# Feed-forward and output products turned around: operand stationary, weights moving in 512 columns

## The chip, the cores and the metric

The kernel runs on one core of a Trainium2 chip. The core has TensorE (PE in the profile, with its weight loads shown as PEld), VectorE (DVE), ScalarE (ACT), GpSimd (POOL) and SyncE (SP, which here only issues DMAs). Times are device microseconds. The kernel before took 1064.02 us, the median of 3 runs (1062.18 to 1064.86). "Faster" and "slower" below mean against that median.

## The reference

A two-layer decoder trunk over 256 tokens of width 1024, all in float32:

```
x = x + 0.5 * ffn(rmsnorm(x))          # f0
x = x + mamba2_mixer(rmsnorm(x))       # ssm: 32 heads, output product y @ w_out (2048 x 1024)
x = x + 0.5 * ffn(rmsnorm(x))          # f1
k, v = kv(rmsnorm(x))                  # shared keys and values
x = x + 0.5 * ffn(rmsnorm(x))          # f2
x = x + attention(rmsnorm(x), k, v)    # window 128, 16 heads; out @ w_o (1024 x 1024) + b_o
x = x + 0.5 * ffn(rmsnorm(x))          # f3
out = rmsnorm(x)
ffn(h) = (silu(h @ w_gate) * (h @ w_up)) @ w_down      # 1024 -> 2816 -> 1024
```

The weight of each norm is folded into the operand that the next product reads; the factor 1/sqrt(mean square + eps) of each token, called rs, is multiplied in after the product.

## The kernel before

Every weight matrix is cut into units of 512 KB, 128 rows by 1024 numbers, in one fixed order (`ORDER`). There are 341 of them: each of the four feed-forwards has 22 gate, 22 up and 22 down units, the mixer 41 input and 16 output units (`so`), the attention 8 query, 2 value and 8 output units (`ao`), and the keys take 2. `Weights` (lines 110 to 183) streams them: SP loads chunks of two units into four buffers, ACT rounds each unit to float32r (`hi`, line 144), and DVE takes the remainder (`lo`, line 155). Six buffers hold the parts, and `ahead` (line 168) keeps four units ready beyond the one in use. The activations are split in the same way, so each product is three: hi by hi, hi by lo, lo by hi.

Activations are kept transposed, with columns on partitions and the 256 tokens along the free dimension: the residual is eight tiles `X` of 128 by 256. In `unit` (line 334, the matmul at 344) and `rows` (line 353, matmuls at 361 to 363) a 128x128 block of the weights is the stationary operand and 256 tokens move, so that a unit is 24 matmuls of 256 columns. In `ffn` (line 456) a gate and an up unit share a PSUM bank; `evac` multiplies by rs (broadcast over partitions), applies SiLU, multiplies and splits into `hh`, `hl` (lines 470 to 479). A down unit follows four tiles later (`LAG`), accumulating into four banks.

`Slots` (line 185) holds the order of the side work by hand: after every unit `tick` runs what was put at that slot, then splits more weights. Each engine runs its instructions in the program's order. The last two units of a product go column tile by column tile in `tail` (line 506), and `next_stage` (line 367) follows each tile with the residual (line 381, or 379 with the attention's bias), the next operand's split (lines 383 and 373) and the squares (line 291, summed on POOL at 294). `stage_norm` (line 449) then sums the squares on TensorE (line 304), takes the root on POOL (lines 313 to 317) and spreads it over partitions with a diagonal (lines 324, 329, 331). `finish` (line 424) is the last norm. In the attention, `rope` (line 802) uses rs, DVE and two POOL operations (815 and 818), and `restack` moves the result by eight DMAs on SP's queue before the scores (line 885) can run; line 966 transposes the probabilities.

Of the kernel before, what the change touches and what calls it, by code (L numbers as in the profile page):

```python
# [9 lines left out]
F32 = mybir.dt.float32  # L10
# [6 lines left out]
P = 128  # L17
# [4 lines left out]
LAG = 4  # L22
SLACK = 2
# the mixer's plan, in slots: by group, by pair of head tiles
# [14 lines left out]
def ffn_order(l, i):  # L39
    o = []  # L40
    for f in range(NF):
        o += [("g", l, i, f), ("u", l, i, f)]
        if l == 1 and i == 0 and f == 5:
            o += [("kA",), ("kB",)]
        if f >= LAG:
            o.append(("d", l, i, f - LAG))
    return o + [("d", l, i, f) for f in range(NF - LAG, NF)]

# [31 lines left out]
# columns of the packed small parameters  # L80
SM = {}
_n = 0
for _name, _w in [
    ("convw", 96), ("convb", 24), ("snw", 16), ("sd", 16),
    ("dtb", 32), ("alog", 32), ("bk", 2), ("bq", 8), ("bo", 8), ("sink", 16), ("bv", 256),
]:
    SM[_name] = (_n, _n + _w)
    _n += _w
NSM = _n

# columns of the norms' weights
NO = {"norm": 0, "kvn": 48, "fin": 56}
NNO = 64

# columns of the constants
# [14 lines left out]
class Weights:  # L110
    """The stream of weight units: loaded in chunks, split into two parts that float32r holds exactly."""
# [56 lines left out]
    def ahead(self, n):  # L168
        """Both parts of the next n units, and the high part of one more."""
# [46 lines left out]
class Trunk:  # L216
    def __init__(self, ctx, tc, a):
# [12 lines left out]
        xp = [cp.tile([P, 2, T], F32, name=f"X{k}") for k in range(KT // 2)]  # L230
        self.X = [xp[k // 2][:, k % 2] for k in range(KT)]
        self.xh = [cp.tile([P, T], F32R, name=f"xh{k}") for k in range(KT)]
        self.xl = [cp.tile([P, T], F32R, name=f"xl{k}") for k in range(KT)]
# [9 lines left out]
        def first(t):  # L243
            q, h = nc.sync.dma_start, D // 2
            q(self.norms, a["norms"])
            q(xp[0], a["x"][:, 0:2, :])
            q(t[:, 0, :h], a["w"][0, :, 0, :h])
            q(xp[1], a["x"][:, 2:4, :])
            q(xp[2], a["x"][:, 4:6, :])
            q(t[:, 0, h:], a["w"][0, :, 0, h:])  # L250
            q(xp[3], a["x"][:, 6:8, :])
            for i in range(1, CH):
                q(t[:, i, :], a["w"][0, :, i, :])

        self.norms = cp.tile([P, NNO], F32, name="norms")
        self.W.load(first)
        self.W.load()
        nc.sync.dma_start(self.co, a["const"])
        self.W.load()
        nc.sync.dma_start(self.sm, a["small"])  # L260
        for _ in range(RAW - 3):
            self.W.load()
        self.ident = self.cc("ident")
        self.slots = Slots()

# [12 lines left out]
    def bank(self, name):  # L278
        return self.ps.tile([P, 512], F32, tag="pp", name=name)

    def accs(self, name):
        return [self.ps.tile([P, 512], F32, tag="acc", name=f"{name}{b}") for b in range(4)]
# [14 lines left out]
    def rs_stats(self, accs, n, key):  # L297
        """1/sqrt(mean + eps) of each token, tokens on partitions; then as diagonals for rs_spread."""
# [3 lines left out]
        for t in range(2):  # L302
            for i, acc in enumerate(accs):
# [3 lines left out]
                )  # L307
        v = wk.tile([P, 2], F32, tag="v", name=f"v_{key}")
        y = wk.tile([P, 2], F32, tag="y", name=f"y_{key}")
        q = wk.tile([P, 2], F32, tag="nt", name=f"nt_{key}")  # L310
        G = nc.gpsimd
        nc.vector.tensor_scalar(v, b[:, 256:258], 1.0 / n, EPS, ALU.mult, ALU.add)
# [5 lines left out]
        return b, y  # L318
# [15 lines left out]
    def unit(self, what, out, xh=None, xl=None, before=None):  # L334
        """A column tile of a product: out[128 columns, tokens] from all eight row tiles."""
        nc = self.nc
        xh = self.xh if xh is None else xh
        xl = self.xl if xl is None else xl
        hi, lo = self.W.next(what)
        passes = [(k, w, x) for k in range(KT) for w, x in ((hi, xh), (hi, xl), (lo, xh))]  # L340
        if self.W.pos == 1:
            passes = [(k, w, x) for w, x in ((hi, xh), (lo, xh), (hi, xl)) for k in range(KT)]
        for n, (k, w, x) in enumerate(passes):
            nc.tensor.matmul(out, w[:, k * P : (k + 1) * P], x[k], start=n == 0, stop=n == len(passes) - 1)  # L344
        if before:
            before()
        self.tick()

# [4 lines left out]
    def rows(self, units, accs, first, last, done=None):  # L353
        """Row tiles of a product, accumulated over all eight column tiles; units: (weights' parts, hh, hl)."""
        nc = self.nc
        for j in range(KT):
            out = accs[j % 4][:, (j // 4) * T : (j // 4) * T + T]
            s = slice(j * P, (j + 1) * P)
            for n, ((hi, lo), hh, hl) in enumerate(units):
                f, e = first and n == 0, last and n == len(units) - 1  # L360
                nc.tensor.matmul(out, hi[:, s], hh, start=f and j < 4, stop=False, skip_group_check=True)  # L361
                nc.tensor.matmul(out, lo[:, s], hh, start=False, stop=False, skip_group_check=True)  # L362
                nc.tensor.matmul(out, hi[:, s], hl, start=False, stop=e, skip_group_check=True)  # L363
            if done:
                done(j, out)

    def next_stage(self, key, scale, wcol, bias=None):
# [9 lines left out]
        def done(j, out):  # L377
# [7 lines left out]
            if j > 0:  # L385
                fin(j - 1)
# [814 lines left out]
```

## Time and profile before

| | |
|---|---|
| median of 3 runs | 1064.02 us |
| the profiled execution's span | 1060.6 us |
| what lies around the span, from the median | 3.4 us |
| TensorE busy, matmuls recorded | 1042.4 us (98%), 8690 |
| VectorE, ScalarE, GpSimd busy | 713.7, 563.9, 79.7 us |
| read from HBM | 187.27 MB, 178 GB/s over the span |
| TensorE's mean granted clock | 0.996 |

The profiled execution has no separate time of its own beside its span; the difference to the median is taken as constant. Busy time of TensorE is modelled, since matmuls are pipelined: a record lasts longer than the distance to the next one. What one matmul costs in a stream is therefore read from the distance between starts, not from its duration. A plain float32 matmul leaves two records, a float32r matmul and a transpose one.

### The profile page before, as it was taken

Reading aid. Unit: us, or ns where it says so; the run is one execution under the profiler, and the core shown is the slowest. Engines: PE = TensorE matmul, PEld = TensorE weight load, DVE = VectorE, ACT = ScalarE, POOL = GpSimd, SP = SyncE. Lnnn points to the kernel's source line nnn. Section 1 sums busy time; section 2 is a strip of 40 time slices with the busy share of each in tenths; the row PEclk is TensorE's granted clock in tenths of the full one; section 3 lists DMA queues with packets and bytes.
Section 4 is the critical chain, followed back from the end, with each engine's and each line's share of the span. In section 5 each row is a group of like instructions: output and inputs, shape, how many; then the busy total and the mean of one; then the engine's idle time right before and its main releaser. Section 6 shows DMA issues by size and latency. Waiting matters only on the chain.

```text
span 1060.6 us, 20911 instructions
## 1 busy us (share of the span) xinstructions
PE 1042.4 (98%) x8690; PEld 1027.5 (97%) x8690; DVE 713.7 (67%) x1245; ACT 563.9 (53%) x930; POOL 79.7 (8%) x122
## 2 busy tenths in 40 slices
PE   8999999999999999999999999999999999999996
PEld 8999999999999999999999999999998899999996
DVE  4755555789999967655556775555589776555554
ACT  6544444669796755444445654444465764444443
POOL 3000000210111111000000200000022020000000
PEclk9999999999999999999999999999999999999998
DMA  8545555457545455455545454555444244555521
GB/s 329 204 170 191 194 191 186 159 180 271 183 151 198 162 193 187 174 190 193 193 166 205 154 200 177 192 190 191 173 178 160 102 159 163 196 181 189 193 94 40
DMA packets 30142, 191.02 MB, mean 180 GB/s; under 512 B 3904, under 2 KB 5728, under 8 KB 8544
## 3 DMA queue, kind: packets, MB, share of 16 engines
q1 hardware_dynamic: 30048, 189.69, 49.0%
q8 instruction: 68, 1.11, 0.4%
q14 instruction: 26, 0.21, 0.1%
HBM read 187.27 MB, written 1.10 MB: 178 GB/s over the span
## 4 chain that ended last, share of the span: by engine, by line
PE 84%; DVE 9%; ACT 3%; DMA 1%; POOL 1%; issue 1%; SPq 1%; DVEq 0%; POOLq 0%
PE gu_f L344 46%; PE da_f L361 8%; PE da_f L362 8%; PE da_f L363 8%; PE sb L344 3%; DVE lo L155 2%; PE q L344 1%; PE sa L361 1%; PE sa L363 1%; PE sa L362 1%; DVE xs L567 1%; DVE E L689 1%; ACT E L684 1%; ACT hi L144 1%; DMA raw<-w 1%
## 5 line engine op out<-in xcount | busy, mean ns | idle before, releaser
L155 DVE TENSOR_TENSOR lo<-raw,hi 128x1024 fp32r<-128x1024 f32 (+1 forms) x343 | 415.4, 1216 | 17.3 <-ACT hi L144 17.2
L344 PE MATMUL gu_f<-xh,hi 128*128 128x256 f32 x1408 | 396.9, 282 | 1.0 <-ACT hi L144 0.9
L344 PE MATMUL gu_f<-xl,hi 128*128 128x256 f32 x1408 | 394.9, 281 | 0.2
L344 PE MATMUL gu_f<-xh,lo 128*128 128x256 f32 x1408 | 394.2, 281 | 0.0
L144 ACT ACTIVATE hi<-raw 128x1024 fp32r<-128x1024 f32 (+1 forms) x343 | 348.4, 1042 | 25.6 <-PE da_f L363 9.8
L344 PEld LDWEIGHTS gu_f<-xh,hi 128*128 128x128 f32 x1408 | 265.1, 188 | 1.8 <-ACT hi L144 1.1
L344 PEld LDWEIGHTS gu_f<-xl,hi 128*128 128x128 f32 x1408 | 265.2, 189 | 1.1 <-DVE xl L373 0.8
L344 PEld LDWEIGHTS gu_f<-xh,lo 128*128 128x128 f32 x1408 | 265.2, 189 | 0.0
L470 DVE TENSOR_TENSOR g_f<-gu_f,rs_f 128x256 f32<-128x256 f32 x88 | 37.3, 424 | 271.8 <-PE gu_f L344 269.2
L471 ACT ACTIVATE g_f<-g_f 128x256 f32<-128x256 f32 x88 | 36.8, 418 | 332.3 <-DVE g_f L470 323.1
L361 PE MATMUL da_f<-hh_f,hi 128*128 128x256 f32 x704 | 198.8, 282 | 0.0
L362 PE MATMUL da_f<-hh_f,lo 128*128 128x256 f32 x704 | 198.7, 282 | 0.0
L363 PE MATMUL da_f<-hl_f,hi 128*128 128x256 f32 x704 | 198.7, 282 | 0.0
L362 PEld LDWEIGHTS da_f<-hh_f,lo 128*128 128x128 f32 x704 | 134.3, 191 | 0.0
L363 PEld LDWEIGHTS da_f<-hl_f,hi 128*128 128x128 f32 x704 | 134.3, 191 | 0.0
L361 PEld LDWEIGHTS da_f<-hh_f,hi 128*128 128x128 f32 x704 | 134.2, 191 | 0.0
L344 PE MATMUL sb<-xh,hi 128*128 128x256 f32 x328 | 94.9, 289 | 0.0
L344 PE MATMUL sb<-xl,hi 128*128 128x256 f32 x328 | 93.0, 283 | 0.0
L344 PE MATMUL sb<-xh,lo 128*128 128x256 f32 x328 | 92.7, 283 | 0.0
L294 POOL TENSOR_TENSOR ss_n<-ss_n,sq_n 128x256 f32<-128x256 f32 x30 | 24.2, 805 | 542.6 <-ACT sq_n L291 540.7
L344 PEld LDWEIGHTS sb<-xh,hi 128*128 128x128 f32 x328 | 62.6, 191 | 0.8 <-issue 0.5
L344 PEld LDWEIGHTS sb<-xl,hi 128*128 128x128 f32 x328 | 62.6, 191 | 0.3 <-DVE xl L373 0.2
(245 smaller groups left out, 1218.3 us busy)
## 6 DMA issues: line engine op xcount, KB each, us to landing
raw<-w SPq DMA_DIRECT2D x168, 1024.0 KB, 4.8
csb<-cs_scratch SPq DMA_DIRECT2D x8, 768.0 KB, 6.9
raw<-w SPq DMA_DIRECT2D x4, 512.0 KB, 7.2
X<-x SPq DMA_DIRECT2D x4, 256.0 KB, 5.5
Q<-r_q SPq DMA_DIRECT2D x32, 32.0 KB, 1.9
out<-o SPq DMA_DIRECT2D x3, 256.0 KB, 2.1
ca<-const_att SPq DMA_DIRECT2D x1, 704.0 KB, 4.1
raw<-w SPq DMA_DIRECT2D x2, 256.0 KB, 5.1
```

Source lines behind the costliest of these rows:

```text
L144: self.nc.scalar.activation(hi[:, s], self.chunks[c][:, i, s], AF.Copy)
L155: self.nc.vector.tensor_tensor(lo[:, s], self.chunks[c][:, i, s], hi[:, s].bitcast(F32), ALU.subtract)
L294: nc.gpsimd.tensor_tensor(self.acc_sq, self.acc_sq, q, ALU.add)
L344: nc.tensor.matmul(out, w[:, k * P : (k + 1) * P], x[k], start=n == 0, stop=n == len(passes) - 1)
L361: nc.tensor.matmul(out, hi[:, s], hh, start=f and j < 4, stop=False, skip_group_check=True)
L362: nc.tensor.matmul(out, lo[:, s], hh, start=False, stop=False, skip_group_check=True)
L363: nc.tensor.matmul(out, hi[:, s], hl, start=False, stop=e, skip_group_check=True)
L470: nc.vector.tensor_tensor(g, b[:, 0:T], self.rs, ALU.mult)
L471: nc.scalar.activation(g, g, AF.Silu)
L567: V.scalar_tensor_tensor(out, u[:, tap : tap + T], self.s("convw", tap * 24 + c), out, ALU.mult, ALU.add)
L684: A.activation(e, e, AF.Exp, scale=-1.0)
L689: V.tensor_tensor(f, f, c, ALU.mult)
```

## The change

The feed-forward products and the output products of the mixer and the attention swap their operands: a 128x128 tile of the activation becomes stationary and 512 weight columns move. Results come out with tokens on partitions. So the residual `X` is now two tiles of 128 tokens by 1024, rs is a number per partition in these products, and both the SwiGLU result and the residual are transposed on TensorE before the next product. The mixer's input products and the query and key products keep the old form. The down units now follow all gate and up units of their feed-forward, and gate and up are done in blocks of 512 columns (four units each). The squares are summed by ScalarE's accumulator; the spread over partitions remains for ssm, f2 and the attention. The attention's bias is added to X on POOL, and the start loads x twice, transposed and by tokens.

```
+    def triple(self, out, x, w, start, stop):
+        mm = self.nc.tensor.matmul
+        mm(out, x[0], w[0], start=start, stop=False)
+        mm(out, x[0], w[1], start=False, stop=False)
+        mm(out, x[1], w[0], start=False, stop=stop)
+        self.filler()                      # one waiting transpose, if there is any
...
+    def block(self, whats, outs):
+        tok = lambda k, t: [self.xs[k][:, i, t * P : (t + 1) * P] for i in range(2)]
+        half = lambda parts, i: [p[:, i * FB : (i + 1) * FB] for p in parts]
+        def part(n, parts, t, i):
+            k = 2 * n + i
+            self.triple(outs[t], tok(k, t), half(parts, i), k == 0, k == KT - 1)
+        if not self.fresh:
...                                         # by unit: 2 row tiles x 2 token halves, then tick
+        got = [self.W.next(what) for what in whats]
+        for t in range(2):                 # first block of a stage: all of t = 0 first
+            for n, parts in enumerate(got):
+                if t == 0 and n == 1:
+                    self.fresh()
+                    self.fresh = None
...
+    def rows(self, units, accs, first):
+        for parts, pair in units:
+            for t in range(2):
+                x = [pair[:, i, t * P : (t + 1) * P] for i in range(2)]
+                for h in range(2):
+                    self.triple(accs[2 * t + h], x, [p[:, h * FB : (h + 1) * FB] for p in parts], first, False)
+    def tail(self, units, accs, nxt):
...
+        for n, (t, h) in enumerate(order):
...                                         # 6 matmuls of 512 columns into accs[2 * t + h]
+            if n:
+                for turn in nxt.turn(*order[n - 1]):
+                    turn()
+            nxt.done(t, h, acc)
+            if n:
+                nxt.split(*order[n - 1])
+        self.fresh = nxt.last
+        self.W.ahead(self.NPART - 2)
...
+    def stage_norm(self, key, spread=False):
+        def h0():
...
+            for t in range(2):
+                for h in range(2):
+                    x = self.X[t][:, h * FB : (h + 1) * FB]
+                    nc.scalar.activation(junk, x, AF.Square, accum_out=ss[:, h, t : t + 1])
+            nc.vector.tensor_tensor(ss[:, 0], ss[:, 0], ss[:, 1], ALU.add)
+            self.rtok = self.rsqrt(ss[:, 0], D, key)
...
+        self.slots.at(0, h0)
+        if spread:
+            self.slots.at(1, h1)           # rs_diag
+            self.slots.late(2, h2)         # rs_spread
...
+        def gate(b, outs, n, g):
+            for t in range(2):
+                nc.scalar.activation(g[t][:, :n], outs[t][:, :n], AF.Silu, scale=self.rtok[:, t : t + 1])
+        def up(b, outs, n, g, h):
...                                         # scalar_tensor_tensor: (up * rtok) * g
+        def turn(b, p, h, tag):            # four 128x128 transposes into one bank, one after each triple
...
+                    self.fill.append(lambda o=o, x=x: nc.tensor.transpose(o, x, self.ident))
+            def split():
+                self.flush()
+                nc.scalar.activation(hp[:, :, 0], v, AF.Copy)
+                nc.vector.tensor_tensor(hp[:, :, 1], v, hp[:, :, 0].bitcast(F32), ALU.subtract)
+            sl.at(1, split)
...
+    def add_bias(self):                    # attention, slot 1
+        for t in range(2):
+            self.nc.gpsimd.tensor_tensor(self.X[t], self.X[t], self.bo, ALU.add)
...
+    def start(self):
...                                         # SP queue: norms, xt0, w0 (2 halves), xt1, w1, xt2, xt3, w2, w3,
...                                         # X (2 x 512 KB), const, w4-5, small, w6-7
+class Boundary:
+    def done(self, t, h, acc):             # X[t][:, half h] += scale * acc, 128x512, DVE
+    def turn(self, t, h):                  # four 128x128 transposes of that half into one bank
+    def split(self, t, h):
...
+        for i in range(4):
+            k, v = 4 * h + i, b[:, i * P : (i + 1) * P]
+            nc.scalar.activation(self.xs[k][:, 0, c], v, AF.Copy, scale=self.wcol(k))
+            nc.vector.scalar_tensor_tensor(
+                self.xs[k][:, 1, c], v, self.wcol(k), self.xs[k][:, 0, c].bitcast(F32), ALU.mult, ALU.subtract
+            )
+    def last(self):                        # turn and split of the order's last (t, h)
```

In the mixer and the attention `unit` calls `self.fresh` in the middle of its first unit (before the fifth of eight row tiles), and their tails go column half by column half. `split_k` in f2 transposes X once more for the keys (16 transposes, 16 pairs of splits). `finish` does for each token half: residual (DVE, 512), square with sum (ACT, 512), the root by logarithm and exponential (ACT) with its correction (DVE, one column), then the two output halves (DVE, 512) with a DMA each.

## Rows read from the trace of the kernel before

**Rows 1.** The page: busy time, granted clock in tenths by slice, chain by engine.

```profile
PE 1042.4 (98%) x8690; PEld 1027.5 (97%) x8690; DVE 713.7 (67%) x1245; ACT 563.9 (53%) x930; POOL 79.7 (8%) x122
...
PEclk9999999999999999999999999999999999999998
...
PE 84%; DVE 9%; ACT 3%; DMA 1%; POOL 1%; issue 1%; SPq 1%; DVEq 0%; POOLq 0%
```

**Rows 2.** Windows: busy us (instructions) of PE, PEld, DVE, ACT, POOL; clock, DMA share, GB/s.

```profile
0.00:20.00 20.00, 17.07 (x111) 16.00 (x111) 8.60 (x15) 12.64 (x25) 6.78 (x12) 1.00 0.88 322
...
410.00:580.00 170.00, 170.00 (x1434) 170.00 (x1433) 100.77 (x147) 75.96 (x104) 0.00 (x0) 1.00 0.51 185
...
790.00:820.00 30.00, 28.86 (x239) 26.88 (x238) 28.84 (x84) 15.97 (x43) 6.68 (x6) 1.00 0.48 167
```

**Rows 3.** Chain that ended last, in order of time: start, us, engine, tile, line.

```profile
26.56 0.43 PE st_f L329 x2
...
400.94 0.79 PE st_f L304 x8
...
430.69 5.68 PE gu_f L344 x48
...
567.43 5.68 PE gu_f L344 x48
```

**Rows 4.** Timeline of PE, the norm's sums: start us, us, line, operation.

```profile
203.99 0.36 PE L304 MATMUL st_ssm<-ones,sq_n 128*128 128x1 f32 x2
...
204.43 0.36 PE L304 MATMUL st_ssm<-ones,sq_n 128*128 128x1 f32 x2
```

**Rows 5.** Timeline of PE at the end, and line 430's durations (min/median/max ns).

```profile
1049.23 1.89 PE L430 MATMUL fin<-last_sq,ones 128*128 128x256 f32 x8
...
L430 PE MATMUL fin<-last_sq,ones x8: 377/379/379, 1049.2 to 1050.7; 128*128 128x256 f32 x8
```

**Rows 6.** Timeline of PE around two runs of transposes, and line 966's durations.

```profile
820.26 1.61 PE L966 MATMUL t<-co,S 128*128 128x128 f32 x12
...
832.60 1.74 PE L966 MATMUL t<-co,S 128*128 128x128 f32 x12
...
834.09 0.36 PE L361 MATMUL aa<-oh,hi 128*128 128x256 f32 x1
...
L966 PE MATMUL t<-co,S x48: 272/273/332, 820.3 to 846.0; 128*128 128x128 f32 x48
```

**Rows 7.** Groups by shape: busy us, mean ns of one, idle time before and its releaser.

```profile
L155 DVE TENSOR_TENSOR lo<-raw,hi 128x1024 fp32r<-128x1024 f32 x339 | 412.7, 1222 | 10.7 <-ACT hi L144 10.7
...
L144 ACT ACTIVATE hi<-raw 128x1024 fp32r<-128x1024 f32 x339 | 346.0, 1047 | 25.2 <-PE da_f L363 9.8 <-PE sa L363 5.0 <-PE q L344 4.0
...
L913 ACT ACTIVATE S<-S,nm 128x128 f32<-128x128 f32 x16 | 6.2, 390 | 8.9 <-DVE nm L906 8.9
...
L923 DVE TENSOR_SCALAR S<-S,sme 128x128 f32<-128x128 f32 x16 | 4.5, 282 | 0.2
```

**Rows 8.** Timeline of POOL in the attention; what PE waited for at the scores.

```profile
787.14 1.61 POOL L313 TENSOR_TENSOR y_att<-v_att,mhalf 128x2 f32<-128x2 f32 x1 [1.90 <-DVE v_att L312]
...
789.66 0.20 POOL L317 TENSOR_TENSOR y_att<-y_att,nt_att 128x2 f32<-128x2 f32 x1
...
795.20 0.86 POOL L815 TENSOR_TENSOR r_q<-rac_q,rbs_q 128x256 f32<-128x256 f32 x1 [5.35 <-DVE rbs_q L813]
...
796.42 1.65 POOL L818 TENSOR_TENSOR r_q<-rbc_q,ras_q 128x256 f32<-128x256 f32 x1 [0.36 <-DVE ras_q L817]
...
PE s L885 <- DMA Q<-r_q: 1.1, 2, 0.9
```

**Rows 9.** Timeline at the end: the last product's matmul, the last VectorE group.

```profile
1049.11 0.28 PE L363 MATMUL da_f<-hl_f,hi 128*128 128x256 f32 x1
...
1053.89 2.77 DVE L444 TENSOR_TENSOR o<-last,fin 128x256 f32<-128x256 f32 x8
```

**Rows 10.** Timeline of the weight loads where the second unit of the kernel begins.

```profile
12.83 0.19 PEld L344 LDWEIGHTS gu_f<-xh,hi 128*128 128x128 f32 x1
```

More of the change, by code (lines that the diff above doesn't have):

```diff
@@ L241, in __init__ @@
         nc.scalar.activation(warm, self.ones[:, 0:1], AF.Silu)
[L243 to L253, printed above, removed]
-        self.norms = cp.tile([P, NNO], F32, name="norms")
[L256 to L262, printed above, removed]
+        self.norms = cp.tile([P, NNO], F32, name="norms")
         self.ident = self.cc("ident")
         self.slots = Slots()
+        self.fill = []
+        self.fresh = None
     def nw(self, name, i):
@@ L332, in rs_spread, with filler, flush, unit @@
         return rs
-    def unit(self, what, out, xh=None, xl=None, before=None):
+    def filler(self):
+        if self.fill:
+            self.fill.pop(0)()
+    def flush(self):
+        while self.fill:
+            self.filler()
[4 more added lines that the diff above has]
+        mm(out, x[1], w[0], start=False, stop=stop)
+        self.filler()
+    def unit(self, what, out, xs=None, before=None):
         nc = self.nc
-        xh = self.xh if xh is None else xh
-        xl = self.xl if xl is None else xl
+        xs = self.xs if xs is None else xs
         hi, lo = self.W.next(what)
[L340 to L344, printed above, removed]
+        passes = [(k, w, i) for k in range(KT) for w, i in ((hi, 0), (hi, 1), (lo, 0))]
+        for n, (k, w, i) in enumerate(passes):
+            if k == KT // 2 and n % 3 == 0 and self.fresh:
+                self.fresh()
+                self.fresh = None
+            nc.tensor.matmul(out, w[:, k * P : (k + 1) * P], xs[k][:, i], start=n == 0, stop=n == len(passes) - 1)
         if before:
@@ L351, in tick @@
         self.W.ahead(self.NPART - 2)
-    def rows(self, units, accs, first, last, done=None):
-        nc = self.nc
[L356 to L365, printed above, removed]
@@ new lines, in tail @@
+    def tail(self, units, accs, nxt):
+        nc = self.nc
+        self.W.ahead(self.NPART - 1)
+        got = [(self.W.next(w), pair) for w, pair in units]
+        while self.slots.todo:
+            self.slots.run()
+        self.flush()
+        order = nxt.order
+        for n, (t, h) in enumerate(order):
+            acc = accs[2 * t + h]
+            for m, (parts, pair) in enumerate(got):
+                w = [p[:, h * FB : (h + 1) * FB] for p in parts]
+                x = [pair[:, i, t * P : (t + 1) * P] for i in range(2)]
+                e = m == len(got) - 1
+                for k, (i, j) in enumerate(((0, 0), (0, 1), (1, 0))):
+                    nc.tensor.matmul(acc, x[i], w[j], start=False, stop=e and k == 2)
+            if n:
[6 more added lines that the diff above has]
+        self.W.ahead(self.NPART - 2)
@@ L1198 @@
     r = _run(nc, [arrays], core_ids=[0])
[L1199 to L1200 removed]
+    return np.asarray(r.results[0]["out"]).reshape(1, T, D)
```

453 lines of the change are left out of this document (240 added, 213 removed).

## The prediction, made before the changed kernel was run

> **What bounds the kernel now.** I read the page's busy time and chain first. TensorE is busy 98% of the span at full granted clock, and 84% of the chain that ended last is TensorE [rows 1]. Busy time alone proves little, since records overlap, so I went to the windows: inside a feed-forward TensorE and its weight loads fill 170.00 of 170.00 us, while VectorE uses 100.8 and ScalarE 76.0, and the DMA engines 51% [rows 2]. So there the end is set by how fast TensorE takes matmuls. Only the attention has a stretch where VectorE (28.84 of 30 us) and TensorE (28.86) are both nearly full [rows 2].
>
> The pace comes from the chain in order of time. The same group of 48 matmuls (a gate and an up unit) takes 5.68 us, 0.1183 us each, and recurs from 430.69 to 567.43 in 16 steps, so gate, up and down take 8.546 us; the down unit is the difference, 2.866 us [rows 3].
>
> What sets 0.118? Three neighbours tell. A matmul of one column still takes its 128x128 weight load, and four of them lie 0.44 us apart, 0.110 each [rows 4]: that is a load's pace with nothing to stream. 256 columns at 2.4 GHz are 0.107 us. So load and stream are nearly equal, and the pace is just above both. The last norm's float32 matmuls send 256 columns twice per record, each with its load: (1.89 - 0.378) / 7 = 0.216 us for 512 columns' worth [rows 5], which is 512 / 2.4 GHz = 0.213 plus 3 ns. Under a stream that long the load disappears. This is the nearest row to the new matmul, and I take 0.216. The ends are 0.213 (clock alone) and 0.237 (two of today's, if something other than the load limits 256 columns, such as reading the moving operand).
>
> The Trainium skill, "TensorE: Matmul & The Clock Gate", section "Back-to-back issue gap", gives N / 2.4 + 2.5 ns for an isolated matmul: 109 ns for 256 columns, 216 for 512. By that rule today's pair costs 218 and turning it saves 3456 x 2.6 ns = 9 us (an estimate from that page), too little to pay for the transposes. The trace disagrees at 256 (118.3 ns, rows 3), where the load shows, and agrees at 512 worth of columns; the measurement decides.
>
> **The change part by part.** Made against the profiled span of 1060.6 us; the median lies 3.4 us above it and I carry that over.
>
> 1. Products. Turned are 264 feed-forward, 16 `so` and 8 `ao` units. Before: 88 x 8.546 + 24 x 2.866 = 820.8 us. After: 288 x 12 = 3456 matmuls x 0.216 = 746.5. **-74.3** (between -84.7 and -1.7).
>
> 2. Transposes. Each feed-forward turns 22 tiles of h for two token halves, 44 in all, so 176; five boundaries turn X with 16 each, the keys once more: 96. Sum 272. Two runs of twelve transposes took (1.61 - 0.273) / 11 = 0.122 and (1.74 - 0.273) / 11 = 0.133 us apiece, the latter with a wait for its bank [rows 6]. The second run ended at 834.34, and the float32r matmul behind it at 834.45, so going back to float32r costs nothing extra. One between two long matmuls has its load hidden but pushes the next load against its own short stream, so I take 0.12: **+32.6** (0.055 for half-hidden to 0.17: 15 to 46).
>
> 3. The norms' sums leave TensorE: six groups of eight one-column matmuls at 0.79 us and three spreads at 0.43 [rows 3]: **-6.0**. Their replacement, four squares of 512 with a sum (about 0.8 each from ScalarE's 390 ns for 128 and 1047 for 1024 [rows 7]), then the root on POOL, lies under the first block, 48 matmuls or 10.4 us. Without that cover some 6 us per stage would show.
>
> 4. Side work in the feed-forwards. Per block of eight units VectorE splits weights, 8 x 1.222, plus four operations of 512 at about 0.69 (between 282 ns for 128 and 1222 for 1024 [rows 7]): 12.5 us; ScalarE 8 x 1.047 plus four at about 0.6: 10.8. TensorE needs 96 x 0.216 + 16 x 0.12 = 22.7. Both fit: **0**. If the up results came late, the transposes queued behind the next unit's first triple would stop TensorE; a whole unit (2.6 us) lies before that. Weights flow at 512 KB per 2.6 us, 202 GB/s, against 322 at the start [rows 2].
>
> 5. Boundaries. Per quarter of the tail TensorE needs 6 x 0.216 + 4 x 0.12 = 1.78 us, VectorE 0.69 + 4 x 0.28 to 0.35 = 1.8 to 2.1, ScalarE 4 x 0.39. VectorE falls a little behind. Before a feed-forward the first token half (24 matmuls, 5.2 us) covers that: 0. Into the mixer and the attention the last quarter is needed in the middle of the first unit, and its splits stand behind a weight split of 1.22 us on VectorE: I work out a stop of 2.3 us against 0.3 now: **+4** for both (0 to +8).
>
> 6. The attention's bias. `add_bias` puts two 128x1024 additions on POOL behind the root, which ends at 789.86, and in front of rope's first operation, now at 795.20; as eight pieces of 256 columns at 0.86 to 1.65 us [rows 8] that is 6.9 to 13.2 us, past 795.20 by 1.6 to 7.9. Behind rope wait its DMAs, then the scores, where TensorE already waits 1.1 us [rows 8], so the delay lands on the path. It also holds SP's queue, but four chunks of weights are loaded by then. **+4** (0 to +11).
>
> 7. Start. Now the second unit begins at 12.83 [rows 10], a loss of 10.0 us before a 2.84 us unit. New: the first matmuls need two of eight row tiles. But 5.2 MB instead of 4.2 stand in SP's queue up to the fifth unit's weights, 16 us at 322 GB/s [rows 2], which can stop TensorE there for up to 3 us. **-1.5** (-3 to +4).
>
> 8. End. From the last product's matmul at 1049.11 to the span's end 11.5 us pass, 3.9 of them behind the last VectorE operation (1056.66) [rows 9]. New, for the last token half: matmul 0.4, residual 0.7, square 0.9, seven one-column steps at about 0.2, two outputs 1.4, and the same 3.9: 8.9 with latencies. **-2.6** (-4 to 0).
>
> Sum: -74.3 + 32.6 - 6.0 + 0 + 4 + 4 - 1.5 - 2.6 = -43.8. Span 1016.8, time **1020 us**, 4.1% faster.
>
> **Rivals.**
> - A fixed cost. If 0.118 is 0.107 of stream plus 11.6 ns that every float32r matmul pays, 512 columns take 0.225: 3456 x 0.009 = +31, 1051 us. For it: float32r differs from the float32 of rows 5. Against: one column takes 0.110 too [rows 4], which a stream plus 12 ns would not.
> - No gain from width (the other side). If the moving operand cannot be read faster than 256 columns in 0.118 us, 512 take 0.2375, item 1 falls to nothing and the transposes remain: +74.3, 1094 us, 3% slower. It decides from 0.216 + 43.8 / 3456 = 0.229 us per matmul. For it: no float32r row is wider than 256. Against: 0.118 is also what a load at 0.110 explains.
> - Lone transposes cost their whole record. A record lasts 0.273 us [rows 6]; if a single transpose between long matmuls is not pipelined, 272 x 0.153 = +41.6 and the time is 1062, no change. Against: the matmul behind the run ended 0.11 after it. The Trainium skill, "TensorE: Matmul & The Clock Gate", section "Part 4: PE-mode transpose", states about 275 ns in one kernel's context; the record here lasts as long, the distance is half.
> - New waits add up: items 5 to 7 at their bad ends, +4, +7 and +5.5: about 1037.
>
> **How the numbers follow.** Forecast 0.74, waits 0.09, fixed cost 0.08, no gain from width 0.06, whole transposes 0.03. The range 1003 to 1040 takes the forecast with 0.213 to 0.220 per matmul (-10 to +14) and transposes from 0.06 to 0.14, and the case of the waits. A difference under 0.3% (3.2 us) cannot be told from no change. Faster: 0.74 + 0.09 + 0.08 = 0.91; same 0.03; slower 0.06.
>
> **What would show it.** In the changed profile 48 matmuls of a block without transposes should take 10.4 us; one transpose between should add 0.12. TensorE's windows should stay full in all feed-forwards, about 178 us each instead of 189.5. The scores' wait should grow past 1.1 us with POOL's additions before it. The prediction is wrong if the pace per 512 columns is above 0.22, or if TensorE shows idle time inside the feed-forwards.

## The result and the profile after

The changed kernel takes 1101.76 us (median of 4 runs, 1100.54 to 1103.49) against 1063.81 for the kernel before beside it: ratio 1.0363, 95% interval 1.0348 to 1.0378. It is 3.6% slower where 4.1% faster was forecast. The profiled span is 1099.5 us; 1016.8 was forecast, so 82.7 us have to be found.

First the page of the changed kernel: busy time, granted clock by slice, chain by engine (against [rows 1]).

```profile
PE 1057.4 (96%) x5444; PEld 876.9 (80%) x5444; DVE 662.8 (60%) x1008; ACT 570.1 (52%) x884; POOL 60.6 (6%) x88
...
PEclk9999999899999999999999999999988999999999
...
PE 76%; DVE 12%; ACT 6%; DMA 2%; issue 1%; POOL 1%; SPq 0%; DVEq 0%; POOLq 0%; ACTq 0%
```

TensorE is as busy as before with 5444 instructions in place of 8690, and VectorE and ScalarE together have grown from 12% of the chain to 18%. So there are two losses to look for: longer matmuls, and new waits. Windows of the changed kernel tell where each is (us, then busy us and instructions of PE, PEld, DVE, ACT, POOL; clock, DMA share, GB/s; against [rows 2]):

```profile
0.00:20.00 20.00, 17.43 (x80) 14.31 (x81) 8.39 (x14) 9.48 (x16) 0.32 (x6) 1.00 0.87 312
...
420.00:600.00 180.00, 180.00 (x807) 145.94 (x806) 94.48 (x95) 82.16 (x96) 5.31 (x5) 1.00 0.55 193
590.00:620.00 30.00, 24.54 (x106) 18.92 (x105) 16.24 (x31) 15.29 (x32) 1.46 (x5) 0.94 0.23 84
800.00:830.00 30.00, 25.44 (x145) 21.74 (x144) 17.33 (x28) 14.99 (x32) 7.03 (x7) 0.89 0.27 95
```

Inside a feed-forward (420 to 600) nothing waits: TensorE fills 180.00 of 180.00 us at full clock. What is lost there is pace. The two windows at boundaries (590 to 620, 800 to 830) have 5.5 and 4.6 us without TensorE and a lower clock.

**The pace.** Timeline of TensorE in the changed kernel, a block (xs stands) and the rows of a down product (hs stands); columns are start us, us, line, operation. Records overlap, so only the distance of starts counts.

```profile
469.14 0.39 PE L331 MATMUL u_f<-hi,xs 128*128 128x512 f32 x1
...
469.84 0.40 PE L331 MATMUL u_f<-hi,xs 128*128 128x512 f32 x1
...
540.37 0.39 PE L331 MATMUL da_f<-hi,hs_f 128*128 128x512 f32 x1
...
541.05 0.39 PE L331 MATMUL da_f<-hi,hs_f 128*128 128x512 f32 x1
```

Line 331 starts every triple, so three matmuls take 0.70 us in the block, 0.2333 each, and 0.68 in the rows, 0.2267 each. Both are flat over whole units. The forecast had 0.216.

**The transposes.** The same timeline where transposes stand between triples:

```profile
542.42 0.27 PE L522 MATMUL ht_f<-co,h_f 128*128 128x128 f32 x1
...
543.22 0.27 PE L522 MATMUL ht_f<-co,h_f 128*128 128x128 f32 x1
...
544.02 0.27 PE L522 MATMUL ht_f<-co,h_f 128*128 128x128 f32 x1
```

The period is 0.80 us: a triple of 0.68 and a transpose of 0.12, though the record lasts 0.27.

**The boundaries.** Timelines of ScalarE, VectorE and TensorE between the feed-forwards f1 and f2: the split of one quarter of X (L1191 rounds a transposed tile, L1192 takes the remainder), and the transposes of two quarters (L1181).

```profile
604.52 0.37 ACT L1191 ACTIVATE xs<-x_n,norms 128x128 fp32r<-128x128 f32 x1 [1.02 <-DVE xs L1192]
605.31 0.37 ACT L1191 ACTIVATE xs<-x_n,norms 128x128 fp32r<-128x128 f32 x1 [0.42 <-DVE xs L1192]
...
604.92 0.35 DVE L1192 SCALAR_TENSOR_TENSOR xs<-x_n,norms,xs 128x128 fp32r<-128x128 f32 x1 [0.43 <-ACT xs L1191]
605.71 0.35 DVE L1192 SCALAR_TENSOR_TENSOR xs<-x_n,norms,xs 128x128 fp32r<-128x128 f32 x1 [0.44 <-ACT xs L1191]
...
601.07 0.66 PE L1181 MATMUL x_n<-co,X 128*128 128x128 f32 x4 [0.59 <-DVE X L1173]
604.28 0.66 PE L1181 MATMUL x_n<-co,X 128*128 128x128 f32 x4 [1.16 <-DVE X L1173]
```

Each engine waits for the other at every tile of a quarter, and there they never overlap (604.52 + 0.37 = 604.89, then 604.92). The rounding of a tile is released by VectorE's remainder of the tile before, though it reads other columns and writes another tile; what the two have in common is the PSUM bank that holds the quarter. Where the banks differ they do overlap:

```profile
599.66 0.62 ACT L1191 ACTIVATE xs<-x_n,norms 128x128 fp32r<-128x128 f32 x2 [0.42 <-DVE xs L1192]
...
600.07 0.35 DVE L1192 SCALAR_TENSOR_TENSOR xs<-x_n,norms,xs 128x128 fp32r<-128x128 f32 x1 [0.43 <-ACT xs L1191]
```

The second of these two roundings (from 599.93) is the first tile of the next quarter, in another bank, and runs beside the remainder of the last tile of this one. A tile takes 0.79 us and a quarter 3.2 (604.28 - 601.07). What it costs TensorE (us in total, times, longest):

```profile
PE x_n L1181 <- DVE X L1173: 4.7, 6, 1.2
PE u_f L332 <- DVE lo L156: 3.9, 1, 3.9
PE st_f L315 <- DVE dg_f L310: 3.7, 1, 3.7
...
PE sb L346 <- ACT xs L1191: 2.8, 1, 2.8
PE q L346 <- ACT xs L1191: 2.8, 1, 2.8
PE s L930 <- POOL r_q L864: 1.9, 1, 1.9
PE x_n L1181 <- DVE X L1171: 1.8, 2, 1.1
```

And TensorE's timeline behind the stop of 3.7 us at st_f:

```profile
616.96 0.63 PE L332 MATMUL g_f<-lo,xs 128*128 128x512 f32 x1
617.38 0.63 PE L333 MATMUL g_f<-hi,xs 128*128 128x512 f32 x1
```

Behind some of the stops the granted clock is at the lower of its levels (0.5, 1.2 GHz) for 3.4 or 6.8 us, and a matmul takes 0.42. Ahead of the end the kernel before has one such stretch of 3.4 us, the changed one six with 30.7 us together.

### The profile page after: what moved, and what is told of

It reads as the page before. It is cut to its first block, busy times and chain, and to the rows that moved or that the text cites. A ratio compares the mean times of both kernels' runs of the same rounds, so it can differ in the third digit from the quotient of the medians.

```text
span 1099.5 us, 13967 instructions
## 1 busy us (share of the span) xinstructions
PE 1057.4 (96%) x5444; PEld 876.9 (80%) x5444; DVE 662.8 (60%) x1008; ACT 570.1 (52%) x884; POOL 60.6 (6%) x88
## 4 chain that ended last, share of the span: by engine, by line
PE 76%; DVE 12%; ACT 6%; DMA 2%; issue 1%; POOL 1%; SPq 0%; DVEq 0%; POOLq 0%; ACTq 0%
PE g_f L332 7%; PE g_f L333 7%; PE g_f L331 7%; PE da_f L331 7%; PE da_f L332 7%; PE da_f L333 7%; PE u_f L332 7%; PE u_f L333 7%; PE u_f L331 7%; DVE lo L156 3%; PE sb L346 3%; DVE xs L1192 2%; ACT xs L1191 2%; PE ht_f L522 2%; DMA raw<-w 2%
## 5 line engine op out<-in xcount | busy, mean ns | idle before, releaser
L331 PE MATMUL g_f<-hi,xs 128*128 128x512 f32 x384 | 159.9, 416 | 0.0
L332 PE MATMUL g_f<-lo,xs 128*128 128x512 f32 x384 | 152.8, 398 | 1.7 <-DVE lo L156 1.5
L333 PE MATMUL g_f<-hi,xs 128*128 128x512 f32 x384 | 152.1, 396 | 0.0
L332 PE MATMUL u_f<-lo,xs 128*128 128x512 f32 x320 | 127.0, 397 | 3.9 <-DVE lo L156 3.9
L331 PE MATMUL da_f<-hi,hs_f 128*128 128x512 f32 x328 | 129.2, 394 | 0.0
L331 PE MATMUL u_f<-hi,xs 128*128 128x512 f32 x320 | 128.4, 401 | 0.0
L333 PE MATMUL da_f<-hi,hs_f 128*128 128x512 f32 x328 | 127.9, 390 | 0.0
L332 PE MATMUL da_f<-lo,hs_f 128*128 128x512 f32 x328 | 127.7, 389 | 0.0
L333 PE MATMUL u_f<-hi,xs 128*128 128x512 f32 x320 | 126.8, 396 | 0.0
L346 PE MATMUL sb<-xs,hi 128*128 128x256 f32 x656 | 124.1, 290 | 2.8 <-ACT xs L1191 2.8
L346 PEld LDWEIGHTS sb<-xs,hi 128*128 128x128 f32 x656 | 103.7, 193 | 5.1 <-ACT xs L1191 3.0
L346 PE MATMUL sb<-xs,lo 128*128 128x256 f32 x328 | 93.3, 285 | 0.0
L331 PEld LDWEIGHTS g_f<-hi,xs 128*128 128x128 f32 x384 | 72.4, 189 | 19.5 <-ACT hi L145 0.8
L333 PEld LDWEIGHTS g_f<-hi,xs 128*128 128x128 f32 x384 | 72.5, 189 | 17.5
```

Source lines behind the costliest of these rows:

```text
L331: mm(out, x[0], w[0], start=start, stop=False)
L332: mm(out, x[0], w[1], start=False, stop=False)
L333: mm(out, x[1], w[0], start=False, stop=stop)
L346: nc.tensor.matmul(out, w[:, k * P : (k + 1) * P], xs[k][:, i], start=n == 0, stop=n == len(passes) - 1)
```

## The experiments

**1. Matmuls alone.** A kernel without the trunk: segments of 48 float32r matmuls with one thing altered in each.

```
L83 block order, two banks    L90 rows order, four banks    L97, L105 other tiles stand
L113 one bank    L117 one tile stands, one slice moves    L140 zeros    L157 VectorE, ScalarE busy
L125 384 columns    L133 256 columns    L148 bf16, 512 columns
```

> A bench that computes none of the trunk: TensorE alone runs streams of 48 float32r matmuls (one line of code for each stream), with VectorE, ScalarE and the DMA queues quiet, then one stream of 96 with VectorE and ScalarE busy. Streams: 256 columns in the old form; 512 in the block's order (two banks in turn) and in the rows' order (four banks), each with two sets of stationary tiles; 512 in one bank; 512 with one tile standing throughout; 384 and 256 columns in the block's order; zeros; bf16. The changed kernel showed 0.2333 us per matmul in its blocks and 0.2267 in its down products, where 0.216 was forecast. Theory F, a fixed cost of 11 to 20 ns on every float32r matmul whatever its width: 256, 384 and 512 columns at about 0.120, 0.173 and 0.227 to 0.233 (a straight line of 0.417 ns per column with a positive intercept), bf16 at 0.216, zeros as the rest. Theory R, the moving operand is read at 0.456 ns per column: 0.117, 0.175, 0.233 for 256, 384 and 512, a line through nothing, the same in every order. Theory C, other engines' traffic costs it: 0.216 in all quiet streams and 0.227 or more in the last one alone. Theory D, the data's power: zeros at 0.216, the others not. Theory A, order or place of the operands: the block's and the rows' order differ here too (0.233 against 0.227), or the two sets of stationary tiles do.

Groups by line (ns of one min/median/max, first to last start in us). From the first to the last start of a segment are 47 steps.

```profile
L83 PE MATMUL bk<-hi,xs x32: 389/389/396, 27.2 to 37.9; 128*128 128x512 f32 x32
...
L117 PE MATMUL bk<-hi,xs x48: 389/389/389, 81.6 to 92.3; 128*128 128x512 f32 x48
...
L125 PE MATMUL bk<-hi,xs x32: 333/334/346, 92.5 to 100.7; 128*128 128x384 f32 x32
...
L133 PE MATMUL bk<-hi,xs x32: 278/283/283, 100.8 to 106.5; 128*128 128x256 f32 x32
...
L148 PE MATMUL bk<-wb,xb x48: 379/379/390, 117.5 to 127.6; 128*128 128x512 bf16 x48
```

From the unrounded starts: 0.1197 us for 256 columns, 0.1739 for 384, 0.2267 for 512 in every order, bank and tile, with zeros too, and 0.2161 in bf16. With VectorE and ScalarE busy beside it (L157) the distance is 0.227 as well, but for the first steps. 256 columns more cost 0.1070, which is 256 / 2.4 GHz (0.1067); so in this bench a float32r matmul costs its columns plus about 13 ns at all three widths (13.0, 13.9, 13.3). In bf16 the rest is 2.8 ns. That is the fixed cost of the first rival. What the blocks take beyond it (0.2333) is not in this bench, and whether the 13 ns hold for tiles at other places experiment 5 will tell. Its segment of the form before (L75) was spoiled by waits at the start.

**2. The boundary in two passes.** ScalarE rounds four tiles, then VectorE takes four remainders.

```
+        for i in range(4):
+            k, v = 4 * h + i, b[:, i * P : (i + 1) * P]
```

> The changed kernel, with the boundary's split in two passes: four ScalarE copies, then four VectorE remainders, instead of copy, remainder, copy, remainder from one PSUM bank. Theory S, that the two engines hand the bank to each other at every tile (the trace of the changed kernel has 0.79 us per tile, of which ScalarE waits 0.42 for VectorE): a quarter's split takes about 1.9 us instead of 3.1, the 20 of the five boundaries end earlier, TensorE's idle time there falls from about 3 us each to under 1, and the clock stays at its upper level in most of them: 10 to 20 us less than the changed kernel, 1082 to 1092 us. Rival, that the splits hide under the tail and the first block: within 3 us of 1101.8.

1076.84 us, ratio 1.0133 (1.0118 to 1.0148): 24 us less than the changed kernel, more than expected. Timelines of ScalarE and VectorE show four tiles in one piece now:

```profile
593.97 1.14 ACT L1191 ACTIVATE xs<-x_n,norms 128x128 fp32r<-128x128 f32 x4 [0.69 <-PE x_n L1181]
...
595.14 1.13 DVE L1194 SCALAR_TENSOR_TENSOR xs<-x_n,norms,xs 128x128 fp32r<-128x128 f32 x4
```

The waits at x_n and st_f are gone, and those at sb and q fell from 2.8 to 1.6 each (1.0 for VectorE, 0.6 for ScalarE): 12.6 us less. The stretches at the lower clock fell from 30.7 to 10.2 us, which at half the clock is worth some 10 us. The two together come near the 24, and this is why the gain is larger than the waits.

**3. The spread of f2's norm four slots later**, on top of experiment 2.

```
+            d = 4 if key == "f2" else 0
-            self.slots.at(1, h1)
-            self.slots.late(2, h2)
+            self.slots.at(d + 1, h1)
+            self.slots.late(d + 2, h2)
```

> The kernel of e2_two_pass, and in f2 alone the diagonal and the spread of rs four slots later (they are needed only by the keys, sixteen slots on). Theory: in the changed kernel TensorE stood 3.66 us at the spread in f2's first block, because its factor was not there and the matmuls of the block are queued behind it, and then ran some 3.4 us at the lower clock: 4 to 6 us less than e2_two_pass. Rival, that the split in two passes already makes the factor early enough: under 1 us less.

1077.59 us, ratio 1.014 (1.0123 to 1.0157): no gain, as the rival said. The wait of 3.7 us at st_f is absent in experiment 2 already: it had come from the late splits and had gone with them.

**4. Places in the SBUF.** What differs between a block and the rows, and between xs and hs, is where the tiles lie. Matmuls only, with tiles put by byte offset:

```
xa 27744 (xs of the changed kernel)   xb 44160   xc 147744 (its hs)   weights a 86304.. (its parts)   b 164160..
```

> What is open: in the changed kernel the 512-column matmuls of the blocks (xs stands, weights move) follow one another at 0.2333 us, those of the rows (hs, yp, op stand) at 0.2267; in the kernel before, 256-column matmuls with xs moving came at 0.117 and with hh, hl moving at 0.120. The first bench had 0.2267 for both orders, with its tiles at other places in the SBUF. This one has only matmuls, no trunk: token tiles xa at the byte offset of the changed kernel's xs (27744), xb at 44160, xc at that of its hs (147744); weights a at the offsets of its weight parts (86304 to 135456), weights b at 164160. Each segment is 48 matmuls of 512 columns in the block order or the rows order, or 96 of 256 columns in the form before. Theory P (the place of the two operands in the SBUF sets the fixed part): block xa a 0.2333, block xc a 0.2267, rows xa a 0.2333, rows xc a 0.2267, old xa a 0.117, old xc a 0.120. Theory A (only whether an offset is a multiple of 64 bytes): xa and xc alike (both are 32 over), xb with weights b different from both. Theory O (the order of the block or what goes on beside it in the kernel): all 512-column segments 0.2267, all 256-column segments 0.120, whatever the place.

Groups by line; block with xa, block with xc, then the form before with xa and with xc, all with weights a (47 steps in the first two, 95 in the others):

```profile
L74 PE MATMUL bk<-ha,xa x32: 393/396/404, 64.8 to 75.7; 128*128 128x512 f32 x32
...
L84 PE MATMUL bk<-ha,xc x32: 388/389/395, 87.2 to 97.9; 128*128 128x512 f32 x32
...
L118 PE MATMUL bk<-xa,ha x64: 279/280/280, 165.0 to 176.1; 128*128 128x256 f32 x64
...
L126 PE MATMUL bk<-xc,ha x64: 280/283/284, 187.8 to 199.1; 128*128 128x256 f32 x64
```

Means of the starts: 0.2335 with xa, 0.2269 with xc, in the rows order 0.2332 and 0.2273; form before 0.1178 and 0.1199. Theory P holds on every count: the block's extra price is a matter of place, and the order is innocent. The cases with xb or weights b that are not shown have 0.2331 to 0.2342 at 512 columns and 0.1178 or 0.1200 at 256. The cases at 0.2267, here and in experiment 1, are those whose stationary and moving slices start alike modulo 256 bytes.

**5. A sweep and a map of the offsets**, both modulo 256 bytes, matmuls only.

```
wide(8 * j, 0)   wide(0, 8 * j)   wide(8 * j, 8 * j)   old(0, 8 * j)   old(8 * j, 0)      # sweep, j < 16
old(8 * i, 8 * j)   wide(8 * i, 8 * j)                                                    # map, i, j < 8
```

> The bench of places had 0.2267 us per 512-column matmul where the stationary and the moving slice start at the same offset modulo 256 bytes (xc 147744 with weights at 86304 and 110880: both 32) and 0.2333 where they don't (xa 96 or xb 128 against 32 or 64), and the form before the other way round: 0.1199 where they agree, 0.1178 where they don't. This one is matmuls only, no trunk: weights and tokens start at multiples of 256 bytes; sweeps of 16 steps of 32 bytes move the stationary slice, the moving slice, or both. Theory M (the difference modulo 256 or 128 bytes sets the fixed part): at difference 0 and again at 128 or 256 the 512-column matmul takes 0.2267, elsewhere up to 0.2333, the same whichever of the two is moved, and flat 0.2267 where both are moved together; the 256-column form 0.120 at 0 and less elsewhere. Theory L (the absolute place decides): moving both together changes the pace as much as moving one.

> The sweeps had one axis at a time; this map takes both offsets in steps of 32 bytes over 256, 24 matmuls for each pair: first the form before (weights stand, 256 token columns move), then 512 weight columns moving. Matmuls only, no trunk. If the difference of the two offsets alone counts, each map is constant along its diagonals: 0.1197 (form before) and 0.2267 (512) on the main one. The sweeps speak for some place counting too: with the moving slice at 192 and the stationary one at 0 the form before took 0.1137, with the stationary one at 64 and the moving one at 0, the same difference, 0.1178. So for the form before one row or column of the map, and not a whole diagonal, should hold about 0.114. The least value of each map gives the price that a kernel of either form could be laid out for: 5300 matmuls of 256 columns at 0.1137 in place of the 0.119 now is 28 us less, about 1036 for the kernel before.

Mean distance of starts in ns (23 steps each), stationary slice at 0, moving slice at 0, 32, ... 224 bytes; then two rows of the map further down:

```
512 columns   at   0: 227.1 233.5 229.3 233.9 233.5 234.0 233.5 233.1
512 columns   at 128: 233.5 234.1 233.5 233.1 227.7 233.4 229.3 233.9
256 columns   at   0: 119.4 118.0 118.0 119.6 118.7 117.4 113.7 118.0
256 columns   at  64: 117.8 118.3 119.7 118.0 118.0 119.6 118.7 117.4
```

The sweep repeats after 256 bytes, and moving both slices together leaves 0.2278: at 512 columns the difference counts, not the place (theory M), and the best difference is 0. At 256 columns the best is 192, with 0.1137 to 0.1147 in five of the eight places of that diagonal, but 0.1176 to 0.1178 in three: neither the whole diagonal, nor the one row or column that was expected. So two matmuls of the old form at their best place (2 x 113.7 = 227.4) cost what one of the new form costs at its best (227).

The map also bounds the 13 ns of experiment 1, where all slices start alike. At a difference of 32 bytes 256 columns take 118.0 and 512 take 233.5, which is 11.3 and 20.2 ns above the columns at 2.4 GHz. Away from equal offsets the price above the columns grows with the width, and two matmuls of the old form (236.0) cost hardly more than one of the new. No run shows what in the chip makes the offsets count.

**6. Equal offsets in the changed kernel**, on top of experiment 2: 64 unused bytes behind xs, which put all later tiles at the offset of xs modulo 256.

```
+        shift = cp.tile([P, 16], F32, name="shift")
+        nc.gpsimd.memset(shift, 0.0)
```

> The changed kernel with the two-pass boundary, and 64 unused bytes per partition behind xs, so that xs (27744) and every tile allocated behind it, the weight parts, hs, op and yp among them, start at the same offset modulo 256 bytes (96). Theory M: the 2112 matmuls of the blocks go from 0.2333 to 0.2267 (2112 x 0.0066 = 14 us off), the 1200 of 256 columns that keep the form before go from 0.117 to 0.120 (3.6 us on), the rows stay at 0.2267: 1077 - 10 = 1066 to 1067 us, ratio to before 1.003. Theory L or another cause in the blocks: 1077, unchanged within 1.5.

1065.31 us, ratio 1.0018 (1.0008 to 1.0028): 12 us less than experiment 2, where theory M had 10. A block in its timeline:

```profile
456.13 0.39 PE L333 MATMUL g_f<-hi,xs 128*128 128x512 f32 x1
...
456.81 0.39 PE L333 MATMUL g_f<-hi,xs 128*128 128x512 f32 x1
```

Three matmuls in 0.68, 0.2267 each, as in the rows.

**7. The kernel before, laid out.** Three unused tiles; weights at 0, every moving token tile at 192 modulo 256.

```
+        self.pad(cp, 16)                       # ahead of xh
+        self.pad(cp, 8)                        # behind xl
+        self.pad(ctx.enter_context(tc.tile_pool(name="behind", bufs=1)), 48)
```

> The kernel before with three unused tiles of 64, 32 and 192 bytes per partition, which put the weight parts at 0 and every token tile that moves (xh, xl, hh, hl, xkh, xkl, yh, yl, oh, ol) at 192 modulo 256 bytes; nothing else is changed. By the map the 256-column matmul takes 0.1137 us there. In the kernel before it took 0.117 to 0.118 (gate and up) and 0.120 (down, keys, values); 5344 of them at a mean of about 0.119: 5344 x 0.0053 = 28 us off, 1036 us, ratio 0.974. If the places in the SBUF counted only in a program without other traffic, it would stay at 1063 (ratio 1.000); if only gate and up go along, about 1048.

1053.44 us (1048.32 to 1057.48), ratio 0.991 (0.9873 to 0.9946): all five runs are below all eight of the kernel before, but the gain is a third of what was expected. Its chain has the group of gate and up at 5.65 us, 8.47 apart with the down unit ([rows 3]: 5.68 and 8.546):

```profile
43.76 5.65 PE gu_f L350 x48
52.23 5.65 PE gu_f L350 x48
```

By stretches of 50 us the mean distance is 0.1178 in most and 0.115 mainly from 200 to 350; before it is 0.118 to 0.119 throughout. Those 150 us are the mixer's input products, whose median is 0.114; gate, up and down have 0.118. So the same pair of offsets can run at 0.1137 or at 0.1178, as the three places on the map's diagonal do. What picks between them stays open.

**8. The start**, on top of experiment 6: the loads of X behind the third pair of weight units, the squares of X two slots later.

```
+        self.W.load()
         for t in range(2):
             nc.sync.dma_start(self.X[t], a["x"][t * P : (t + 1) * P, :])
         nc.sync.dma_start(self.co, a["const"])
-        self.W.load()
...
-        self.slots.at(0, h0)
+        self.slots.at(2 if key == "f0" else 0, h0)
```

> The kernel of e4 (two-pass boundary, equal offsets) with two moves at the start: the two loads of X and that of the constants stand behind the third pair of weight units instead of ahead of it, and the squares of X for the first norm come two slots later. In e4 the weight load of that pair held ACT back 3.9 us, the four squares (2.9 us of ACT) stood ahead of the next rounding, and TensorE waited 4.2 us at the first u_f and then had half its clock for 6.9 us. Theory: the queue order makes the late start; TensorE no longer waits at u_f and keeps its clock, 4 to 7 us off: 1059 to 1061, ratio 0.996. Rival: the bytes and not their order are short, X is loaded in any case, and the wait only moves to the next units: 1064 to 1066, ratio 1.002.

1061.86 us, ratio 0.9976 (0.9967 to 0.9986): by the ratios 4.5 us less than experiment 6, by the medians 3.5. TensorE's wait at u_f fell from 3.9 to 1.9 us and the lower clock behind it from 6.8 to 3.4. So the start was late in part for the order; 1.9 us of the wait stay. The two moves were made together, and no run parts them.

**9. The attention's bias later**, on top of experiment 8. In the changed kernel, the timelines of POOL and VectorE at the start of the attention:

```profile
824.59 4.71 POOL L1071 TENSOR_TENSOR X<-X,row 128x1024 f32<-128x1024 f32 x2 [0.22 <-issue]
833.05 0.92 POOL L864 TENSOR_TENSOR r_q<-rac_q,rbs_q 128x256 f32<-128x256 f32 x1 [3.75 <-DVE rbs_q L862]
...
824.60 2.44 DVE L310 TENSOR_SCALAR dg_att<-co,y_att 128x128 f32<-128x128 f32 x1
826.97 4.55 DVE L156 TENSOR_TENSOR lo<-raw,hi 128x1024 fp32r<-128x1024 f32 x2
```

```
-        sl.at(1, lambda: self.add_bias())
+        sl.late(11, lambda: self.add_bias())
```

> The kernel of e6 with the attention bias's two POOL additions moved from the first slot of the attention to the twelfth (behind the last rope, among the output products). In the changed kernel these additions take 4.71 us from 824.59, and in just that stretch VectorE's operations are long: a 128x128 scaling of dg_att 2.44 us where 0.28 is its usual time, two weight splits 2.28 each where 1.22 is; the queue of POOL itself is empty for 3.75 us before rope's first operation. Theory: while POOL adds large float32 tiles VectorE runs at about half its pace, so the first rope starts some 4 us late and the scores wait 1.7 us for r_q and 1.4 for its DMAs; moved, dg_att takes 0.28, the splits 1.22, and the scores' waits fall below 1 us together: 2 to 4 us off, 1058 to 1060, ratio 0.995. Rival: the durations belong to that place (VectorE behind ScalarE, or the banks) and not to POOL: dg_att and the splits stay long and the time stays at 1061 to 1063, ratio 0.998.

1060.82 us, ratio 0.998 (0.9971 to 0.9989): the time of the rival and the mechanism of the theory. VectorE's timeline and one of TensorE's waits:

```profile
790.38 0.48 DVE L312 TENSOR_SCALAR dg_att<-co,y_att 128x128 f32<-128x128 f32 x2 [1.70 <-POOL y_att L305]
790.78 2.35 DVE L156 TENSOR_TENSOR lo<-raw,hi 128x1024 fp32r<-128x1024 f32 x2
...
PE t L1013 <- DVE S L970: 3.6, 3, 2.9
```

Two scalings take 0.48 us (2.65 in experiment 8), a split 1.18 in place of 2.28, and the scores' waits fell from 3.1 in experiment 8 to 0.6. But the additions now stand beside the third of four softmax groups, and TensorE waits 2.9 us for its scaled S there. The wait was moved, not removed. And it is a block rather than half a pace: in the changed kernel dg_att's second scaling lasts 2.44 us, as long as POOL's first addition (4.71 / 2), and two splits beside the second one take 4.55, which is the 2.33 us until POOL ends (829.30 - 826.97) and two splits of 1.18. The same shows at the new place, in the timelines of POOL and VectorE:

```profile
829.96 4.66 POOL L1073 TENSOR_TENSOR X<-X,row 128x1024 f32<-128x1024 f32 x2
...
832.38 0.21 DVE L966 RECIPROCAL sme<-sme 128x8 f32<-128x8 f32 x1
832.62 2.08 DVE L970 TENSOR_SCALAR S<-S,sme 128x128 f32<-128x128 f32 x1
```

The scaling of S, 0.28 before ([rows 7]), stands until POOL's second addition ends (834.62). The reciprocal ahead of it, under the same addition, does not: not every VectorE operation is held.

## Why the prediction was wrong

The step that failed is item 1, "This is the nearest row to the new matmul, and I take 0.216". The row was float32, the matmul is float32r, and the runs showed 0.2267 to 0.2333 in its place. A second step failed beside it, item 5: the two engines were taken to work side by side on a quarter, and they take turns.

- **Products: -74.3 forecast, -23.4 measured** (2112 x 0.2333 + 1344 x 0.2267 = 797.4 against 820.8). The load was not what set 0.118: with a load each, 256 columns ran at 0.1137 to 0.120 as the offsets were moved. Rows 4 did not speak against this: one column takes 0.110 for its load, which says nothing of what 256 take when the load is hidden. Nor do [rows 5] hold two loads per record, as the prediction had it: the trace has one. The fixed-cost rival got 0.08 and is right for the down and output products, which stand at equal offsets (about 13 ns against its 11.6). In the blocks the width saved next to nothing, 2 x 0.1183 before and 0.2333 after. There the second rival, no gain from width, comes near in size; whether its mechanism, a moving operand read too slowly, is at work no run shows. The place of the tiles added 14 us in the blocks, and so the mean pace (797.4 / 3456 = 0.2307) passed 0.229, from where that rival said the change loses. The rule quoted from the Trainium skill ("TensorE: Matmul & The Clock Gate", "Back-to-back issue gap") agrees with the bf16 row, 2.8 ns measured for its 2.5; for float32r the size is about 13 at equal offsets. The saving estimated from it, 9 us, was called too small to pay for the transposes; the kernel as built saved 23.4, against 32.6 for them.
- **Transposes: +32.6, right where it can be read.** 0.12 apiece between the long matmuls of the feed-forwards, and no whole records.
- **Norms' sums and side work: right but for two stops.** From 420 to 600 us TensorE does not wait, and the one-column matmuls of [rows 3] are gone from the feed-forwards. But it stands 3.9 us at the start of the first and 3.7 at the spread of f2, whose cause is the boundary (experiment 3). The block of 48 took 11.2 us and not 10.4, which is the pace again.
- **Boundaries: +4 forecast; about 24 too little.** I let ScalarE and VectorE run side by side on a quarter (1.8 to 2.1 us). Sharing one bank they take turns, 3.2 us. The stops into the mixer and the attention came nearly as worked out, 2.8 us for 2.3; the stops inside the tails (6.5 us) and at f2's spread had been put at nothing. The Trainium skill, "PSUM — Partial Sum Buffer", section "PSUM bank collisions raise a hardware error", says that two engines must not be on one bank at once; the trace agrees, on one bank the records never overlap, and I had not weighed it. The lost clock behind the stops was not in the sum at all. Experiment 2 gives 24 us back.
- **Attention's bias: a wait was expected, by another way.** POOL's two additions took 4.71 us, not 6.9 to 13.2, and its queue was free 3.75 us before rope; VectorE stood while POOL added. The scores' waits rose from 1.1 to 3.0. The Trainium skill, "SBUF — State Buffer", section "Who interferes with whom", has this: the two share a pair of ports, and for VectorE operations that need the shared pair, who starts first holds it for the whole instruction. The 2.44 us of dg_att agree with it.
- **Start: -1.5 forecast.** The stop at the fifth unit's weights came, 3.9 us and not "up to 3", with the lower clock behind it; experiment 8 gives up to 4.5 back, of which some 1.7 is a longer stretch at the lower clock that experiment 6 had there (6.8 us) and the changed kernel had not (3.4).
- **End: -2.6 forecast, -1.3 measured.** From the last product's matmul to the span's end pass 10.2 us:

```profile
1089.27 0.39 PE L333 MATMUL da_f<-hi,hs_f 128*128 128x512 f32 x1
...
1095.12 1.42 DVE L468 SCALAR_TENSOR_TENSOR o<-X,fin_y,row 128x512 f32<-128x512 f32 x2
```

The terms: 50.9 of pace, 24 at the boundaries, 4.5 at the start, 1.3 at the end, 80.7 of the 82.7 us. They come from different runs and are good to some 3 us, so this shows the order of size and not that nothing else was lost. Mended one by one (experiments 2, 6, 8, 9) the changed kernel comes to 1060.8, 0.2% below the kernel before, which is no change by the prediction's own bound of 0.3%. Of the 41 us that then part it from the forecast, 37 are the fixed cost (3456 x 0.0107) and some 2 the 1224 matmuls of 256 columns that kept the form before (0.1183 there, 0.1199 at equal offsets). So of the 820.8 us before (0.2375 for 512 columns) the width saves 3456 x (0.2375 - 0.2267) = 37 us at equal offsets, and the transposes take back 32.6: that is where the gain went. What is still lost lies mostly in the attention: from its first query matmul to the first gate matmul of f3 pass 76.6 us in the kernel before, 89.7 in the changed one and still 82.9 in experiment 9.

## What to carry to other kernels

Take the pace of a matmul from rows of its own type, at both widths, and with the tiles at the offsets that they will have: only what does not grow with the width is saved by fewer, wider matmuls, 13 ns apiece here at equal offsets and next to nothing elsewhere. Before a product is turned, set that saving against the transposes it needs. And where two engines empty one PSUM bank, give each its whole pass: taking turns made each quarter here 3.2 us long, and TensorE lost its clock behind it.

## What the runs showed of the hardware

- A float32r matmul whose two slices start alike modulo 256 bytes costs its columns at 2.4 GHz plus about 13 ns at 256, 384 and 512 columns; bf16 at 512 plus 2.8 ns.
- Where its stationary and moving slices start modulo 256 bytes changes that: at 512 columns 0.2267 at equal offsets, up to 0.234 elsewhere; at 256 columns 0.1197 at equal offsets, 0.117 to 0.120 at most others and 0.1137 at some with a difference of 192 bytes. Three unused tiles, 288 bytes of each partition, made the kernel before 0.9% faster.
- While POOL adds a 128x1024 float32 tile (2.4 us), a scaling or a subtraction that begins beside it on VectorE stands until it ends: 2.44 us in place of 0.28 for a 128x128 scaling. A reciprocal of 128x8 took 0.21 under the same addition.
- ScalarE and VectorE took turns on one PSUM bank, 0.79 us a tile, and overlapped on two banks.
- Behind some stops, of 1.1 to 3.9 us, TensorE had half its clock for 3.4 or 6.8 us, which is 1.7 or 3.4 us more lost than the wait shows.
